# A hybrid decoder step on one core: head sums in two one-pass halves, banks from the plan, a new order of the mixers

## The chip, the core and the metric

The kernel runs on one core of a Trainium2 chip. The metric is the device time of one execution in microseconds (us). The kernel before took 1525.13 us, the median of three runs (1524.78 to 1525.69).

## What is computed

One layer of a decoder over 272 prompt positions (16 meta tokens and 256) and 8 samples of 4 positions, model width 2048, all in fp32. One input projection feeds two parallel groups, RWKV-7 time mixing (16 heads of 64) and retention (4 heads of 256). Their outputs go through one output projection, a residual addition and a SwiGLU FFN of width 5632.

```
z = rms_norm(x) @ w_in                      # RWKV columns | retention columns
# RWKV: kk = k*k_k / |k*k_k| per head;  S = S*w + (S a) b^T + v k^T;  o = S r
#       o = group_norm(o) per head of 64 + sum(r*k*r_k per head) * v;  o * g
# retention: rotary q, k;  o = (q k^T * decay) v + (q S) * decay;  S = g^C S + k^T v
#       o = o * rsqrt(mean(o*o) per head of 256) * silu(g)
h = x + concat(o_rwkv, o_ret) @ w_out
h = h + (silu(hn @ w_gate) * (hn @ w_up)) @ w_down,   hn = rms_norm(h)
```

It returns the final norms of h for prompt and samples, and the new shift, RWKV and retention states of the prompt and of each sample.

## The kernel before, in words

Activations lie with features on the partitions and tokens along the free axis: 304 tokens in the input projection, 288 from the output projection on (the meta tokens are dropped).

**Weights.** All projection weights lie in one stream `big` of 823 tiles of 128 x 512, in the order of use (`sequence`, L109, and `steps`, L129). A tile is loaded by SyncE's queue into one of five buffers (`load`, L658). ScalarE rounds it to fp32r (`wh`, `cast`, L667), and VectorE subtracts to get the rest (`wl`, `rest`, L682). For each block of 128 x 128 TensorE does three one-pass fp32r matmuls: `wh*xh`, `wh*xl`, `wl*xh` (`main`, L688). A job is one output tile of 128 columns: 16 blocks in the input projection, 8 in each half of the output projection, up to 4 in the down projection. Jobs alternate between two PSUM accumulators (`ACC`); a job starts when one is free and its `need` holds.

**Order.** `ORDER` (L55) says in which order the 56 mixer jobs of the input projection come after three jobs for the low-rank inputs: three per RWKV head pair (`p0` to `p7`), six per retention head (`r0` to `r3`), two per gate (`g0` to `g3`). Then come 16 jobs of the output projection on the RWKV half, 16 on the retention half, and the FFN in groups of four tiles (`FSTEP`): gate and up jobs, then 16 down jobs.

**Streams.** All that isn't the weight stream is written as generators (`pair` L980, `bonus`, `by_token`, `inverse`, `units`, `sample` L1302, `pair_out` L1380, `ret` L1462, and the evacuations of jobs). A `Plan` (L325) runs the whole program once as a draft with its own costs of each instruction, and whenever a stream's last result is due by its clock of TensorE it takes that stream's next step, lowest rank first. So it writes out one fixed program order for each engine; the same decisions are replayed for the real program. If the weight stream can't go on, the plan takes the next stream that comes due. In the profile nearly all instructions have the line of the helper that records them, L314.

**Space.** Scratch tiles get places in one SBUF arena, packed by the lifetimes of the draft (`Room`, L505). Six PSUM banks (`mm`) serve the streams in turn (`ps`, L647).

**Limits on concurrency.** Pair p starts when pair p-2 has passed its inverse (`PAIRS`) and pair p-3 is done (`PMAX`). Retention h starts after pair `RSTART[h]` is done.

**The sums over heads.** The matrix `blk` (128 x 128, ones where two rows are of the same head of 64) is the stationary operand of fp32 matmuls that sum over a head: of the squares of k (312 columns, L1014), of r*k scaled by `rk` (288, L1142), of the sample correlations (320, L1338), and for mean and variance of the output (288 each, L1384 and L1392). In retention two fp32 matmuls with a matrix of ones sum the squares (L1594). An fp32 matmul shows in the trace as two records.

**States of the samples.** `sample` ends with the new state of the 8 samples: a transpose, a 512-column fp32 matmul and an addition into the loaded state. `ret` does so for the retention states, four times two fp32r matmuls of 512 columns per head with two VectorE updates each.

Of the kernel before, what the change touches and what calls it, by code (L numbers as in the profile page):

```python
# [68 lines left out]
for _n, _w in [("id", 128), ("blk", 128), ("mar", 256), ("lvl", 2 * 64), ("m16", 64), ("i16", 16), ("h16", 32), ("h32", 128), ("rst", TP),  # L69
               ("bm128", 8), ("ks", 12), ("kss", 4), ("qs", 128), ("own", 256), ("sel", 32)]:  # L70
    CV[_n] = _o
    _o += _w
# [10 lines left out]
ROOM = 33040  # L83
GAP = 56
WIDE = 4200
# [62 lines left out]
def constants():  # L148
# [48 lines left out]
    put("own", np.tile((np.arange(8)[:, None] == bb[None, :]).astype(f).reshape(1, 256), (P, 1)))  # L197
# [121 lines left out]
class Plan:  # L319
# [5 lines left out]
    def __init__(self, nc, rooms, draft, log, keep):  # L325
# [8 lines left out]
        self.streams, self.made = [], 0  # L334
        self.pe = Timed(self, nc.tensor, "PE")
# [5 lines left out]
    def decide(self, f):  # L341

        if not self.draft:
            return self.log.pop(0)
        self.log.append(f())
        return self.log[-1]

# [14 lines left out]
    def book(self, eng, what, a, k):  # L362
# [40 lines left out]
        for x in aps:  # L403
            for room in self.rooms.values():
                room.use(x, self.count, self.begun if eng == "PE" else self.clock[eng] - 400, done)
        for name, box, writes in boxes:
# [181 lines left out]
class Step:  # L588


    def __init__(self, tc, I, O, ctx, rooms, draft, log):
# [8 lines left out]
        self.pp = pool("psum", 8 - ACC, space=bass.MemoryType.PSUM)  # L600
# [3 lines left out]
        if not draft:  # L604
            self.arena = {dt: self.mp.tile([P, r.size + (GAP if dt == F32 else 0)], dt, tag=f"arena_{dt}", name=f"arena_{dt}")
# [3 lines left out]
        self.outs = []  # L609
        self.live = 0  # L610
        self.done = set()

# [10 lines left out]
    def t(self, shape, tag, dt=F32, bufs=None, pool=None):  # L623
        self.n += 1
        if pool is not None:
            ap = pool.tile(shape, dt, tag=tag, name=f"{tag}_{self.n}", **({} if bufs is None else {"bufs": bufs}))
            if tag in ("mm", "acc"):
                self.plan.banks.add(ap.name)
            old = self.tags.setdefault(tag, [])
            old.append(ap.name)  # L630
            n = {"mm": 8 - ACC, "acc": ACC}.get(tag, bufs)
# [15 lines left out]
    def ps(self):  # L647
        return self.t([P, 512], "mm", pool=self.pp)
# [39 lines left out]
    def main(self, jobs):  # L688
# [3 lines left out]
        accs = {}  # L692
        for key, k in steps():
# [3 lines left out]
            if k == 0:  # L697
# [8 lines left out]
                else:  # L706
                    accs[key] = self.first = self.ps()
# [52 lines left out]
    def rsqrt(self, src, scale, eps, floor=None, out=None):  # L760
# [34 lines left out]
    def start(self):  # L795
# [32 lines left out]
        pt = self.ps()  # L828
# [14 lines left out]
    def constants(self):  # L843
# [6 lines left out]
        self.cst = self.t([P, NCV], "cst", pool=self.cp)  # L850
        self.sp.dma_start(self.cst, I["cst"])
# [5 lines left out]
        for a, n in (8, 4), (2, 2), (1, 1):  # L857
            self.dve.tensor_add(xr[:, :n], xr[:, :n], xr[:, a:a + n])
        yield
        yield  # L860
        ssq = self.ps()
# [118 lines left out]
    def pair(self, p, z):  # L980
        cst, act, dve, pe, pool = self.cv, self.act, self.dve, self.pe, self.pool
        blk = cst("blk", P)
# [9 lines left out]
        pw = self.ps()  # L992
        k, r, v, (wh, wl) = z["k"], z["r"], z["v"], z["lora", 0]
        xw, xa = self.xw
        pa = self.ps()
# [7 lines left out]
        rkb = self.t([P, P], "rkb")  # L1003
        dve.tensor_scalar(rkb, blk, self.pv("rk", p), None, op0=ALU.mult)
# [8 lines left out]
        pn = self.ps()  # L1013
        pe.matmul(pn[:, :TP], blk, sq, start=True, stop=True)  # L1014
# [3 lines left out]
        c = self.t([P, TP], "c")  # L1018
# [864 lines left out]
```

## Time and profile before

| | us |
|---|---|
| median of three runs | 1525.13 |
| the profiled execution | 1525.16 |
| its span, first to last instruction | 1523.3 |
| input projection and mixers, with the first output job at | 583.1 |
| first sum of the FFN's norm (fp32, 1 column) | 697.8 |
| last weight matmul | 1510.1 |

In the profile PE is TensorE's matmuls and PEld its weight loads, DVE is VectorE, ACT ScalarE, POOL GpSimd, SP SyncE. A row of the groups gives engine, operation, output and inputs by the program's names (scratch tiles are `arena_dt.float` or `arena_dt.float32r`, the streams' PSUM banks `mm`, the accumulators `acc`), shapes, count, busy time and mean length, then idle time of the engine before them. Matmul records overlap, since matmuls are pipelined; the distance of their starts is what one takes from the stream.

### The profile page before, as it was taken

What the parts mean: (1) busy time and instruction counts of PE and PEld (TensorE: products, weight loads), DVE (VectorE), ACT (ScalarE), POOL (GpSimd) and SP (SyncE); (2) the same over time, 40 slices, a digit from 0 to 9 for tenths busy, and PEclk for the clock granted to TensorE, in tenths of its full rate; (3) what the DMA queues carried; (4) which work ended last, traced back from release to release, by engine and by line L of the source; (5) the groups of instructions that cost most, each with busy time, mean ns of one, the idle gap of its engine ahead of it and who ended that gap; (6) DMA issues with size and microseconds to landing.
All of it is one profiled execution on the core that took longest, in us unless ns stands there. A gap on an engine that the chain in (4) does not pass through costs nothing.

```text
span 1523.3 us, 31919 instructions
## 1 busy us (share of the span) xinstructions
PE 1506.5 (99%) x11446; PEld 1479.4 (97%) x11446; DVE 1087.7 (71%) x2782; ACT 866.4 (57%) x2031; POOL 27.7 (2%) x161
## 2 busy tenths in 40 slices
PE   9999999999999999999999999999999999999997
PEld 8999999999899998999999999999999999999997
DVE  6989789989989877776665655656565656565657
ACT  6775876787886865555444444444444444444446
POOL 1000000000000000000000000000000000000000
PEclk9999999999999999999999999999999999999998
DMA  7655435434544476665566565555656655555663
GB/s 235 177 142 144 126 109 156 126 116 146 163 129 146 167 235 213 210 181 167 167 172 169 172 172 174 166 173 168 170 171 167 177 174 167 172 169 173 169 176 119
DMA packets 136335, 252.33 MB, mean 166 GB/s; under 512 B 15985, under 2 KB 22257, under 8 KB 136177
## 3 DMA queue, kind: packets, MB, share of 16 engines
q1 hardware_dynamic: 136176, 250.29, 55.4%
q8 instruction: 91, 1.49, 0.4%
q14 instruction: 68, 0.55, 0.1%
HBM read 235.95 MB, written 14.28 MB: 164 GB/s over the span
## 4 chain that ended last, share of the span: by engine, by line
PE 89%; DVE 7%; ACT 2%; issue 1%; DMA 0%; SPq 0%; DVEq 0%; ACTq 0%
PE acc L314 79%; PE mm L314 10%; DVE arena_dt.float L314 5%; DVE wl L314 2%; ACT arena_dt.float L314 1%; DMA arena_dt.float<-xT 0%; ACT wh L314 0%; SPq L314 0%; DVE arena_dt.float32r L314 0%; ACT arena_dt.float32r L314 0%; DVE xl L314 0%; ACT xh L314 0%; DVEq L1879 0%; ACT shout L314 0%; DVEq L314 0%
## 5 line engine op out<-in xcount | busy, mean ns | idle before, releaser
L314 PE MATMUL acc<-xh,wh 128*128 128x288 f32 (+2 forms) x2592 | 787.5, 304 | 2.1 <-ACT wh L314 1.3
L314 PE MATMUL acc<-xh,wl 128*128 128x288 f32 (+2 forms) x2592 | 763.2, 294 | 0.3 <-DVE wl L314 0.3
L314 PE MATMUL acc<-xl,wh 128*128 128x288 f32 (+2 forms) x2592 | 760.1, 293 | 0.1
L314 ACT CAST wh<-wr 128x512 fp32r<-128x512 f32 (+1 forms) x827 | 501.2, 616 | 334.6 <-PE acc L314 297.9
L314 DVE TENSOR_TENSOR wl<-wr,wh 128x512 fp32r<-128x512 f32 (+1 forms) x827 | 559.3, 686 | 125.6 <-ACT wh L314 122.7
L314 PEld LDWEIGHTS acc<-xh,wh 128*128 128x128 f32 x2592 | 486.7, 188 | 9.0 <-issue 3.7
L314 PEld LDWEIGHTS acc<-xl,wh 128*128 128x128 f32 x2592 | 486.2, 188 | 4.5 <-issue 1.2
L314 PEld LDWEIGHTS acc<-xh,wl 128*128 128x128 f32 x2592 | 485.3, 187 | 0.9 <-DVE wl L314 0.6
L314 PE MATMUL acc<-arena_dt.float32r,wh 128*128 128x288 f32 x1408 | 273.1, 292 | 0.4 <-ACT arena_dt.float32r L314 0.3
L314 PEld LDWEIGHTS acc<-arena_dt.float32r,wh 128*128 128x128 f32 x1408 | 223.7, 188 | 0.9 <-ACT arena_dt.float32r L314 0.6
L314 PE MATMUL acc<-arena_dt.float32r,wl 128*128 128x288 f32 x704 | 205.6, 292 | 0.0
L314 DVE TENSOR_TENSOR arena_dt.float<-acc,arena_dt.float 128x288 f32<-128x288 f32 (+4 forms) x181 | 72.8, 420 | 161.7 <-PE acc L314 161.4
L314 DVE TENSOR_TENSOR arena_dt.float<-arena_dt.float 128x288 f32<-128x288 f32 (+22 forms) x694 | 175.4, 287 | 11.9 <-ACT arena_dt.float L314 7.6
L314 ACT ACTIVATE arena_dt.float<-arena_dt.float 128x288 f32<-128x288 f32 (+7 forms) x245 | 104.7, 434 | 114.5 <-DVE arena_dt.float L314 112.6
L314 PE MATMUL mm<-arena_dt.float 128*128 128x128 f32 (+7 forms) x1136 | 167.6, 302 | 0.7 <-issue 0.2
L314 DVE TENSOR_TENSOR arena_dt.float<-arena_dt.float,acc 128x288 f32<-128x288 f32 (+1 forms) x210 | 94.6, 451 | 88.3 <-PE acc L314 87.0
L314 PEld LDWEIGHTS mm<-arena_dt.float 128*128 128x128 f32 (+1 forms) x1136 | 141.3, 181 | 11.4 <-issue 3.9
L314 PEld LDWEIGHTS acc<-arena_dt.float32r,wl 128*128 128x128 f32 x704 | 132.1, 188 | 0.0
L314 ACT COPY arena_dt.float<-mm 64x64 f32<-64x64 f32 (+11 forms) x330 | 91.6, 287 | 48.9 <-PE mm L314 39.9
L314 ACT CAST arena_dt.float32r<-arena_dt.float 128x288 fp32r<-128x288 f32 (+4 forms) x73 | 30.5, 423 | 89.4 <-DVE arena_dt.float L314 88.7
L314 ACT COPY arena_dt.float<-arena_dt.float 128x32 f32<-128x32 f32 (+7 forms) x235 | 57.1, 293 | 13.3 <-DVE arena_dt.float L314 11.5
L314 DVE SCALAR_TENSOR_TENSOR arena_dt.float<-arena_dt.float 128x288 f32<-128x288 f32 (+3 forms) x96 | 43.1, 452 | 2.4 <-ACT arena_dt.float L314 0.5
(66 smaller groups left out, 564.8 us busy)
## 6 DMA issues: line engine op xcount, KB each, us to landing
wr<-big SPq DMA_DIRECT2D x823, 256.0 KB, 2.9
arena_dt.float<-s0r SPq DMA_DIRECT2D x16, 512.0 KB, 5.2
out_rts<-arena_dt.float SPq DMA_DIRECT2D x16, 512.0 KB, 4.5
arena_dt.float<-xT SPq DMA_DIRECT2D x4, 576.0 KB, 4.3
arena_dt.float<-lora SPq DMA_DIRECT2D x16, 128.0 KB, 2.7
arena_dt.float<-s0w SPq DMA_DIRECT2D x8, 256.0 KB, 3.0
out_rws<-arena_dt.float SPq DMA_DIRECT2D x8, 256.0 KB, 3.7
out_y<-arena_dt.float SPq DMA_DIRECT2D x7, 288.0 KB, 2.5
```

What stands on the lines that cost most here:

```text
L314: return self._plan.keep(f(*a, **k))
```

## The change

- **Sums.** `blk`, a matrix of ones and a new matrix `cen` (identity minus the mean over the head) are kept in fp32r. Each sum over a head splits its operand with a ScalarE copy and a VectorE subtraction (`split`) and adds two one-pass fp32r matmuls (`total`). `cen` gives the centred output at once. In retention the two squares are added first, and one sum is left. The bonus scales with `rk` in its product, so the scaled copy of `blk` goes.
- **VectorE.** `dp` (decay up to the token before) is taken from shifted columns of `dd`, with three small ScalarE copies for the first columns; two factors move into neighbouring instructions; the reciprocal root loses its shift; `qz` is cleared by GpSimd and filled by two ScalarE copies, without the mask `own`.
- **Banks.** The plan gives out the six PSUM banks: the one that came free first, among those whose announced uses are over.
- **Order.** Pairs and retentions alternate, gates come last. Three pairs may be ahead of their inverse and four alive; retentions 0 and 1 wait for no pair.
- **Late states.** The sample states of the pairs are updated after the output projection with the state loaded again (`sample_state`, rank 99), those of retention heads 2 and 3 after the last retention (`held_states`, rank 98).
- **Stage seams.** The conversions of the mixer outputs for the output projection follow the last input job block by block (`fill`, `refill`). In the last down group the first two jobs are interleaved, and each block waits for its own activation only.

```
-PAIRS = 2
-PMAX = 3
+PAIRS = 3
+PMAX = 4
+HELD = 2
-RSTART = (3, 5, 6, 6)
-ORDER = "p0 p1 g0 p2 r0 p3 p4 g1 p5 r1 p6 g2 p7 g3 r2 r3"
+RSTART = (-1, -1, 6, 6)
+ORDER = "p0 p1 p2 r0 p3 p4 r1 p5 p6 p7 r2 r3 g0 g1 g2 g3"
-ROOM = 33040
-WIDE = 4200
+ROOM = 33008
+WIDE = 4800
...
-    return first + [(key, k) for key in seq[3:] for k in range(extent(key)[0])]
+    rest = [(key, k) for key in seq[3:-KT] for k in range(extent(key)[0])]
+    n = extent(seq[-1])[0] - 1
+    pair = [(key, k) for key in seq[-KT:2 - KT] for k in range(n)] + [(key, n) for key in seq[-KT:2 - KT]]
+    return first + rest + pair + [(key, k) for key in seq[2 - KT:] for k in range(n + 1)]
...
+    put("cen", np.eye(P, dtype=f) - (r[:, None] // 64 == r[None, :] // 64).astype(f) / f(64))
...
+    def bank(self):
+        held = set(self.at.values())
+        return min((b for b in range(8 - ACC) if b not in held), key=lambda b: self.free[b])
...
-    def ps(self):
-        return self.t([P, 512], "mm", pool=self.pp)
+    def ps(self, uses):
+        b = self.plan.decide(self.plan.bank)
+        return self.t([P, 512], f"mm{b}", pool=self.pp, bufs=1, uses=uses)
...   (main)
+            while key[0] == "down" and k not in j.xs:
+                yield False
...
+            if key == last and ("o", k) in self.done:
+                self.fill(k)
...   (rsqrt)
-        dve.tensor_scalar(a.bitcast(I32), x.bitcast(I32), 1, None, op0=ALU.logical_shift_right)
-        yield
-        dve.tensor_scalar(y.bitcast(I32), a.bitcast(I32), -1, 0x5F1FFFF9, op0=ALU.mult, op1=ALU.add)
+        dve.tensor_scalar(y.bitcast(I32), x.bitcast(I32), -0.5, 0x5F1FFFF9, op0=ALU.mult, op1=ALU.add)
...   (pair)
-        pe.matmul(pn[:, :TP], blk, sq, start=True, stop=True)
+        hl = yield from self.split(sq)
+        pn = self.total(self.blk, hl)
...
-        dve.tensor_mul(ra[:, 0, :], kk, dp)
+        dve.tensor_mul(ra[:, 0, 1:], kk[:, 1:], dd[:, :TP - 1])
+        act.copy(ra[:, 0, :1], kk[:, :1])
+        act.copy(ra[:, 0, UB[1]:NP:64], kk[:, UB[1]:NP:64])
+        act.copy(ra[:, 0, NP + 1::5], kk[:, NP + 1::5])
...
+    def split(self, x):
+        hl = self.t([P, 2, x.shape[1]], "hl", F32R)
+        self.act.copy(hl[:, 0, :], x)
+        yield
+        self.dve.tensor_sub(hl[:, 1, :], x, hl[:, 0, :])
+        return hl
+    def total(self, what, hl, uses=1):
+        pt = self.ps(2 + uses)
+        for i in range(2):
+            self.pe.matmul(pt[:, :hl.shape[2]], what, hl[:, i, :], start=not i, stop=i == 1)
+        return pt
...   (sample)
+        self.later.append(self.sample_state(p, sb, d4))
+    def sample_state(self, p, sb, d4):
+        s0 = self.t([P, NB, 64], "s0n")
+        self.sp.dma_start(s0, self.I["s0w"][p])
...   (pair_out)
-        pe.matmul(pm[:, :TO], cst("blk", P), o, start=True, stop=True)
+        hl = yield from self.split(o)
+        pm = self.total(self.cen, hl, 2)
-        dve.scalar_tensor_tensor(o, pm[:, :TO], -1.0 / 64, o, op0=ALU.mult, op1=ALU.add)
-        act.activation(sq, o, AF.Square)
-        pe.matmul(pn[:, :TO], cst("blk", P), sq, start=True, stop=True)
+        act.activation(sq, pm[:, :TO], AF.Square)
+        act.copy(o, pm[:, :TO])
+        hl = yield from self.split(sq)
+        pn = self.total(self.blk, hl)
...   (ret)
+    def held_states(self, h, ks, vt):
+        skh, svh = yield from self.exact(ks, vt)
+        for b2 in range(NB // 2):
+            s0 = self.t([P, 2, 2, RD], "s0n")
+            self.sp.dma_start(s0, self.I["s0r"][h, b2])
+            yield
+            yield from self.new_state(h, b2, s0, skh, svh)
...
-            self.pe.matmul(pt[:, :TO], self.ones, sq[:, e, :], start=e == 0, stop=e == 1)
+        dve.tensor_add(sq[:, 0, :], sq[:, 0, :], sq[:, 1, :])
+        hl = yield from self.split(sq[:, 0, :])
+        pt = self.total(self.all, hl)
...   (ffn_jobs)
-                                need=lambda f=f1 - 1: ("act", f) in self.done))
+                                need=lambda f=f1 - 1 - (f1 == FT): ("act", f) in self.done))
```

More of the change, by code (lines that the diff above doesn't have):

```diff
@@ L405, in book @@
                 room.use(x, self.count, self.begun if eng == "PE" else self.clock[eng] - 400, done)
+        for name in {x.name for x in aps if x.name in self.left}:
+            self.left[name] -= 1
+            assert self.left[name] >= 0, name
+            if not self.left[name]:
+                self.free[self.at.pop(name)] = done
         for name, box, writes in boxes:
@@ L608, in __init__ @@
         pl.outside = {v.name for v in (*I.values(), *O.values())}
-        self.outs = []
+        self.outs, self.later, self.held = [], [], []
         self.live = 0
         self.done = set()
+        self.filled = set()
     def put(self, dst, src):
@@ L692, in main @@
         accs = {}
+        last = [key for key in sequence() if key[0] == "in"][-1]
         for key, k in steps():
@@ L849, in constants @@
         self.sp.dma_start(self.shin, I["shift"])
-        self.cst = self.t([P, NCV], "cst", pool=self.cp)
-        self.sp.dma_start(self.cst, I["cst"])
+        o, n = CV["blk"], NCV - CV["blk"]
+        self.cst = self.t([P, o], "cst", pool=self.cp)
+        self.sp.dma_start(self.cst, I["cst"][:, :o])
+        raw = self.t([P, n], "sums")
+        self.sp.dma_start(raw, I["cst"][:, o:])
+        sums = self.t([P, P + n], "sums", F32R, pool=self.cp)
+        self.act.copy(sums[:, :P], self.ones)
+        self.all, self.blk, self.cen = (sums[:, c * P:(c + 1) * P] for c in range(3))
         for g in range(0, KT, 4):
@@ L858, in constants @@
             self.dve.tensor_add(xr[:, :n], xr[:, :n], xr[:, a:a + n])
+        self.act.copy(sums[:, P:], raw)
         yield
         yield
-        ssq = self.ps()
+        ssq = self.ps(2)
         self.pe.matmul(ssq[:, :T], self.ones, xr[:, 0, :], start=True, stop=True)
@@ L1336, in sample @@
             yield
-        pt = self.ps()
-        pe.matmul(pt[:, :320], cst("blk", P), cf, start=True, stop=True)
+        hl = yield from self.split(cf)
+        yield
+        pt = self.total(self.blk, hl)
         yield
@@ L1512, in ret @@
         dve.tensor_mul(pr, pt[:, :RMW], rm)
-        qz = self.t([P, 2, NB, 32], "qz")
         for d in range(2):
-            dve.tensor_mul(qz[:, d], qh[:, d, None, :].to_broadcast([P, NB, 32]),
-                           cst("own", 256).rearrange("p (b c) -> p b c", c=32))
-        pt = self.ps()
+            act.copy(qz[:, d, :, :4], four(qh[:, d]))
+        pt = self.ps(7)
         for d in range(2):
@@ L1557, in ret @@
                 act.copy(qo, pt[:, :RD])
[L1559 to L1576 removed]
+            if now:
+                for b2 in range(2 * g, 2 * g + 2):
+                    yield from self.new_state(h, b2, s0s[b2], skh, svh)
+        if not now:
+            self.held.append(self.held_states(h, ks, vt))
+            yield
         ot = self.t([P, 2, TO], "ot")
@@ L1591, in ret @@
         yield
-        pt = self.ps()
-        for e in range(2):
-            pe.matmul(pt[:, :TO], self.ones, sq[:, e, :], start=e == 0, stop=e == 1)
+        dve.tensor_add(sq[:, 0, :], sq[:, 0, :], sq[:, 1, :])
+        yield
+        hl = yield from self.split(sq[:, 0, :])
+        yield
+        pt = self.total(self.all, hl)
         yield
@@ L1600, in ret @@
         self.done.add(("ret", h))
+        if h == RH - 1:
+            self.plan.add(self.rest_of(self.held), 98)
         yield from self.ret_out(h)
@@ L1671, in bridge, with fill, refill @@
     def bridge(self, n=BRIDGE):
-        pt = self.ps()
+        pt = self.ps(n)
         for _ in range(n):
             self.pe.matmul(pt[:, :P], self.ones, self.ones, start=True, stop=True)
+    def fill(self, k):
+        if k not in self.filled:
+            self.filled.add(k)
+            xh, xl = self.xf[k]
+            self.act.copy(xh, self.os[k])
+            self.dve.tensor_sub(xl, self.os[k], xh)
+    def refill(self):
+        for k in range(8, KT):
+            while ("o", k) not in self.done:
+                yield
+            self.fill(k)
+            yield
     def out_jobs(self, half):
@@ L1697, in f @@
                     self.done.add("hs")
+                    self.plan.add(self.rest_of(self.later), 99)
                 yield from self.sumsq(self.ssq2, hm, m == 0)
@@ L1748, in g @@
                 acts[f - f0] = hl[:, 0, :], hl[:, 1, :]
-                if last:
-                    self.done.add(("act", f))
+                self.done.add(("act", f))
             return g
```

189 lines of the change are left out of this document (99 added, 90 removed).

## The prediction

> **What bounds the kernel now.** I read the page's engine table first, then the table of windows by stage, then the groups by form, and last the timeline around single sums. The page, of the one profiled execution:
>
> ```profile
> span 1523.3 us, 31919 instructions
> ...
> PE 1506.5 (99%) x11446; PEld 1479.4 (97%) x11446; DVE 1087.7 (71%) x2782; ACT 866.4 (57%) x2031; POOL 27.7 (2%) x161
> ```
>
> TensorE is busy throughout, but a matmul record also counts pipelined time, so the share alone proves little. The windows say more: the length, then busy time and instructions of PE, weight load, VectorE, ScalarE and GpSimd, then the granted clock, DMA share and rate.
>
> ```profile
> 50.00:550.00 500.00, 498.47 (x3696) 480.68 (x3694) 444.68 (x1577) 381.60 (x1127) 22.26 (x122) 1.00 0.48 143
> 550.00:583.00 33.00, 31.85 (x228) 28.20 (x226) 19.68 (x46) 19.39 (x48) 0.00 (x0) 1.00 0.75 262
> ```
>
> ```profile
> 700.00:1480.00 780.00, 780.00 (x6054) 780.00 (x6053) 467.92 (x842) 338.96 (x594) 0.00 (x0) 1.00 0.59 171
> ```
>
> In the FFN one one-pass matmul of 288 columns starts every 780/6054 = 0.1288 us, without a break, at clock 1.00. Nothing can be won there but fewer passes. In the mixer stage (50 to 583) PE shows 1.53 + 1.15 = 2.7 us of idle time, while VectorE is at 444.68/500 = 89%. So in both stages the passes of TensorE are the time: what is taken off PE comes off the end one for one, as long as its next instruction is always ready. A cheaper VectorE buys nothing by itself; a VectorE that falls behind would cost.
>
> **The sums over heads.** Five per pair go from one fp32 matmul to two one-pass halves: the norm of k (312 columns), the bonus (288), the sample correlations (320), mean and variance in the output (288 each). Per retention head two fp32 matmuls with ones become an addition and one sum in halves. Their groups by form, two records to an fp32 matmul:
>
> ```profile
> L314 PE MATMUL mm<-arena_dt.float,cst 128*128 128x288 f32 x32 | 10.8, 418 | 0.2 <-ACT arena_dt.float L314 0.2
> ...
> L314 PE MATMUL mm<-arena_dt.float,cst 128*128 128x320 f32 x16 | 5.7, 436 | 0.0
> L314 PE MATMUL mm<-arena_dt.float,cst 128*128 128x312 f32 x16 | 5.6, 432 | 0.0
> L314 PE MATMUL mm<-arena_dt.float 128*128 128x288 f32 x16 | 5.5, 423 | 0.1
> ...
> L314 PE MATMUL mm<-arena_dt.float,ones 128*128 128x288 f32 x16 | 4.5, 406 | 0.0
> ```
>
> So 16 output sums, 8 of 320, 8 of 312, 8 bonuses, 8 of ones. The means overlap one another and are no prices. The price is how far a sum puts off the passes behind it, which the timeline shows (start, length, instruction):
>
> ```profile
> 213.66 0.57 PE L314 MATMUL mm<-arena_dt.float32r 128*128 128x288 f32 x3
> 214.06 0.65 PE L314 MATMUL mm<-arena_dt.float,cst 128*128 128x288 f32 x2
> 214.33 0.52 PE L314 MATMUL acc<-xh,wh 128*128 128x304 f32 x1
> 214.69 0.30 PE L314 MATMUL acc<-xl,wh 128*128 128x304 f32 x1
> 214.83 0.30 PE L314 MATMUL acc<-xh,wl 128*128 128x304 f32 x1
> ```
>
> ```profile
> 86.76 0.70 PE L314 MATMUL mm<-arena_dt.float,cst 128*128 128x320 f32 x2
> 87.05 0.54 PE L314 MATMUL acc<-xh,wh 128*128 128x288 f32 x1
> 87.43 0.29 PE L314 MATMUL acc<-xl,wh 128*128 128x288 f32 x1
> ```
>
> ```profile
> 608.68 1.13 PE L314 MATMUL mm<-arena_dt.float,ones 128*128 128x288 f32 x4
> 609.44 0.51 PE L314 MATMUL acc<-xh,wh 128*128 128x288 f32 x1
> 609.79 0.29 PE L314 MATMUL acc<-xl,wh 128*128 128x288 f32 x1
> ```
>
> From the sum's start to the second pass behind it, less the one pass between:
> - 288 columns: 214.69 - 214.06 - 0.14 = 0.49. Two halves: the three one-pass matmuls of 288 from 213.66 to 214.06 take 0.133 each, the FFN 0.129, so 0.26. Saves 0.23, times 24 = 5.5 us.
> - 320: 87.43 - 86.76 - 0.13 = 0.54 against 2 x 0.129 x 320/288 = 0.29. Saves 0.25, times 8 = 2.0. 312 lies between: 0.53 against 0.28, again 0.25, times 8 = 2.0.
> - Ones: 609.79 - 608.68 - 0.13 = 0.98 against 0.26. Saves 0.72, times 4 = 2.9.
>
> Sum: 12.4 us, all on PE, all where PE has no spare time. Mixing the two kinds of matmul costs nothing that shows: the 0.49 holds both changes of kind.
>
> The Trainium skill (FP8 and Floating Point Precision, TensorE Precision Notes) says that true FP32 takes four passes through the array. An estimate by that page would be 4 x 0.129 = 0.515 for the sum whose row gives 0.49, and 13.8 us saved in all instead of 12.4. The trace nearly agrees, at 3.8 passes; the rows decide.
>
> **What the sums add elsewhere.** Each sum now needs a ScalarE copy to the rounded half and a VectorE subtraction before PE may start. Off the path; these rows price VectorE's side:
>
> ```profile
> L314 DVE TENSOR_TENSOR wl<-wr,wh 128x512 fp32r<-128x512 f32 (+1 forms) x827 | 559.3, 686 | 125.6 <-ACT wh L314 122.7
> ...
> L314 DVE TENSOR_TENSOR arena_dt.float<-arena_dt.float,acc 128x288 f32<-128x288 f32 (+1 forms) x210 | 94.6, 451 | 88.3 <-PE acc L314 87.0
> ...
> L314 DVE TENSOR_TENSOR arena_dt.float32r<-arena_dt.float,arena_dt.float32r 128x288 fp32r<-128x288 f32 (+4 forms) x72 | 31.8, 441 | 1.1 <-ACT arena_dt.float32r L314 0.7
> ...
> L314 DVE SCALAR_TENSOR_TENSOR arena_dt.float<-arena_dt.float,mm 128x512 f32<-128x512 f32 x32 | 20.5, 682 | 0.3 <-PE mm L314 0.2
> ```
>
> Five subtractions of 0.44 = 2.2 us a pair come in; six VectorE instructions of a like size go out (scaled mask, dp, the factor of ta, the centring, the shift in two reciprocal roots). I take that as even, so "less VectorE work" is mainly work that leaves the mixer: half of the 32 state updates (heads 2 and 3, 16 x 0.68 = 11 us), plus two instructions of that size per pair (8 x 1.36 = 11 us). VectorE falls from 445 to about 423 of those 500 us. A sum's operands come some 0.9 us later, about 4.5 us a pair. That is hidden: between the last columns of pair 7 and the output projection there are now 20 jobs (two retentions, four gates) of 48 passes, 20 x 48 x 0.129 = 124 us, where there were 14. Eight pairs, two at a time, in 500 us make 125 us for a pair at most. Were the cover gone, the 4.5 us would show once, for the last pair.
>
> **Starts and ends of stages.** At the first output job all eight x tiles were converted at once; in the last FFN group PE waited for the last activation:
>
> ```profile
> 583.09 0.40 PE L314 MATMUL acc<-xh,wh 128*128 128x288 f32 x1 [0.79 <-ACT xh L314]
> 583.58 0.40 PE L314 MATMUL acc<-xl,wh 128*128 128x288 f32 x1
> ```
>
> ```profile
> 1485.43 0.29 PE L314 MATMUL acc<-arena_dt.float32r,wl 128*128 128x288 f32 x1
> 1486.06 0.89 PE L314 MATMUL acc<-arena_dt.float32r,wh 128*128 128x288 f32 x2 [0.34 <-ACT arena_dt.float32r L314]
> 1486.79 0.29 PE L314 MATMUL acc<-arena_dt.float32r,wl 128*128 128x288 f32 x1
> ```
>
> At 583 the loss is 0.79 + (0.49 - 0.13) = 1.15 us. The conversions now follow the last input job tile by tile; I take 1.0 back (bounds 0 and 1.15). At 1486 it is (0.63 - 0.13) + (0.73 - 0.26) = 0.97. With two jobs interleaved, 18 passes stand ahead of the one that needs the last activation, instead of nine, 1.16 us more, so that stall goes. What is late next is the third job: it takes the first one's accumulator, free 0.29 (a pass) + 0.45 (the addition, above) = 0.74 after that job's last pass starts, and is due after 4 x 0.13 = 0.52. Net 0.97 - 0.22: I take 0.7 (bounds 0, if another VectorE instruction of 0.68 stands in front, and 0.97).
>
> **Order, banks, early retention.** These move waits, and the trace of before has few to move. At 1486 0.34 us of idle stood for 0.97 lost, so the 1.53 us shown in 50 to 550 can stand for up to 4.4. I take 0: the changes can remove at most 4.4, and with a third pair and retention from the start more short chains feed PE, each of which can come late by as much; the other end is the VectorE rival below.
>
> **Sample states late.** The matmuls are the same and cost PE the same, in the FFN. Added are reloads on SP's queue: eight of s0w, and eight of s0r for heads 2 and 3.
>
> ```profile
> arena_dt.float<-s0r SPq DMA_DIRECT2D x16, 512.0 KB, 5.2
> ...
> arena_dt.float<-s0w SPq DMA_DIRECT2D x8, 256.0 KB, 3.0
> ```
>
> That is 6.3 MB on queues whose share in the FFN is 0.59. Behind a reload that waits for its place in SBUF stand the weight loads; five buffers of 12 passes are 5 x 1.55 us, so SP may be held about 6 us before PE starves. I take 0; bounds 0, and 0.5 us for each of 16 reloads, 8 us (5.2 + 3.0 of landing against those 6 us leaves 2 at worst, so 0 is the nearer end).
>
> **The sum.** The profiled execution took 1525.16 us, 1.9 around its span, and the median of the runs is 1525.13, so they stand for each other. 1525.1 - 12.4 - 1.0 - 0.7 = 1511.0 us.
>
> **The rivals.**
> - *VectorE becomes the bound while three pairs and retentions 0 and 1 run together (slower).* Up to pair 7's last columns (39 of 59 input jobs, so some 39/59 x 533 = 350 us) 1.5 times the pair work may be wanted at once. Of 445 us in 50 to 550 at most 3696/12 x 0.686 = 211 are weight halves; the other 234 are 0.47 of the time, at 1.5 times 0.70, with the weights 1.12. That puts VectorE 0.12 x 350 = 42 us behind. It decides once the lag exceeds the slack of the other accumulator, one job of 48 passes or 6.2 us. If half of the lag reaches PE, 1511 + 21 = 1532. For it: 89% now. Against: 22 us leave the mixer, and streams that lag give way to input jobs as long as there are any.
> - *The halves save nothing, because weight loads set the pace (no change).* Of the weight loads:
>
> ```profile
> L314 PEld LDWEIGHTS acc<-xh,wh 128*128 128x128 f32 x2592 | 486.7, 188 | 9.0 <-issue 3.7
> ```
>
> Each sum has two loads before and after. At 0.188 a load a sum in halves takes 0.38 when nothing overlaps; if the present 0.49 is likewise set by loads and drains that stay, only the ones sums gain, 8 loads or 1.5 us: 1525.1 - 1.5 = 1523.6. Against: a pass starts every 0.129 us, so loads of 0.188 overlap.
>
> The Trainium skill (Perfetto Trace Analysis, Identifying the Most-Contended Engine) judges TensorE's headroom by weight-load busy share and not by matmul busy share; at 97% that rule speaks against the change. The FFN's spacing of 0.129 says that this share is no limit here.
> - *Late states collide with the weight stream.* 1511 + 8 = 1519.
> - *The short waits go too.* 1511 - 4.4 = 1506.6.
>
> **How the numbers follow.** The forecast has 0.67: with halves at 0.133 the sum is 0.4 smaller, and the two small terms span 0 to 2.1, the unknown waits about 2 either way, so its own range is 1508 to 1515. VectorE 0.09, weight loads 0.06, late states 0.09, short waits 0.09. About 0.2%, 3 us, is what a measurement can tell from no change. Faster: 0.67 + 0.09 + 0.09 = 0.85; same 0.06; slower 0.09. The range 1506 to 1519.5 takes in all but the first two rivals.
>
> **What would show it.** Right: the fp32 groups with cst and with ones over 288 are gone, 44 x 2 one-pass records stand in their place 0.13 apart; 700 to 1480 still gives 0.129 a pass outside the late matmuls; PE idle in 50 to 550 stays near 1.5 us; no 0.79 us ahead of the first output job. Wrong: PE waiting in the mixer on VectorE's results or on accumulators for more than 10 us in all, a first output job that waits for pair 7, or ScalarE's weight copies waiting on wr loads beside s0n reloads.

## The result: 2.7% slower, and where the profile after puts it

The changed kernel took 1565.49 us, the median of four runs (1561.24 to 1570.62), against 1525.03 us for the kernel before: a ratio of 1.0266 (95% interval 1.0235 to 1.0297). The forecast was 1511.0 with a range to 1519.5. The result lies 54 us above the forecast, on the slower side, which had a chance of 0.09. The profiled execution has a span of 1563.9 us, 40.6 more than before.

One remark for the numbers below: two runs of the first experiment (1539.6 and 1540.5 us) and one of the fourth (1586.9 us) are not compared, since the profiled ones among them show FFN passes 3.5% further apart than the profile of after, and the rows of the first experiment's profile are used up to 675 us only, where nothing else is said.

The page after, busy times and the chain that ended last:

```profile
PE 1511.4 (97%) x11438; PEld 1480.9 (95%) x11438; DVE 1092.1 (70%) x2768; ACT 881.5 (56%) x2109; POOL 31.5 (2%) x165
...
PE 82%; DVE 6%; ACT 4%; DMA 4%; issue 2%; SPq 1%; DVEq 0%; ACTq 0%
```

Here the share of a busy engine misleads. PE is still at 97%, and only the chain shows the change: 18% of it is now not PE, with VectorE, ScalarE and DMAs in it. Before, 11% was not PE (89% PE, 7% DVE, 2% ACT, DMA 0%).

The windows by stage, of after, with the columns as in the prediction:

```profile
50.00:550.00 500.00, 476.64 (x3562) 463.25 (x3560) 429.60 (x1528) 366.63 (x1081) 29.04 (x146) 0.99 0.43 135
550.00:675.00 125.00, 115.45 (x855) 107.33 (x854) 82.70 (x174) 68.00 (x157) 0.21 (x1) 0.97 0.64 221
...
800.00:1480.00 680.00, 680.00 (x5278) 680.00 (x5278) 409.51 (x735) 293.12 (x513) 0.00 (x0) 1.00 0.58 171
```

And of before, the one that the prediction did not show and that is needed here:

```profile
550.00:675.00 125.00, 123.66 (x934) 117.42 (x933) 91.35 (x192) 71.66 (x154) 0.00 (x0) 1.00 0.66 216
```

The last row of after shows the FFN untouched: 5278 passes in 680 us, 0.1288 each. The loss is ahead of it. In the 500 us of the mixers PE has 500 - 476.64 = 23.4 us of idle time, where before it had 1.5, and it got 134 records less done (3562 instead of 3696), although each sum is now shorter. VectorE is less busy than before (429.60 instead of 444.68), so by this row it is not the bound. In 550 to 675 idle grows from 1.3 to 9.6 us. By the timeline the first output job starts at 606.9, not 583.1 (+23.8), and the last weight matmul at 1551.3, not 1510.1 (+41.2). The mixers lose more than those 23.8, since the shorter sums and the late states took work out of them; in the 17.4 behind lie the late states, which moved there, and the idle time of the output projection.

What do they wait for? The waits of after (us in total, times, longest):

```profile
ACT wh L317 <- DMA wr<-big: 37.9, 26, 4.1
...
PE mm L317 <- ACT arena_dt.float L317: 11.2, 9, 2.4
...
ACT arena_dt.float32r L317 <- DMA arena_dt.float<-lora: 8.3, 5, 3.4
```

The same waits of before:

```profile
ACT wh L314 <- DMA wr<-big: 5.9, 5, 1.5
...
PE mm L314 <- ACT arena_dt.float L314: 1.1, 3, 0.6
...
ACT arena_dt.float32r L314 <- DMA arena_dt.float<-lora: 0.5, 1, 0.5
```

ScalarE waits 37.9 us for weight tiles (5.9 before), and PE's short matmuls of the streams wait 11.2 us for ScalarE (1.1). But the weights were late to be asked for, rather than slow to come: from issue to landing they take 2.9 us by the page, before and after. The waits of SP's queue, before and then after:

```profile
SPq L314 <- DVE wl L314: 902.6, 700, 13.0
SPq L314 <- DVE arena_dt.float L314: 205.3, 98, 16.6
...
SPq L314 <- PE mm L314: 8.2, 7, 3.5
```

```profile
SPq L317 <- DVE wl L317: 784.4, 638, 6.4
SPq L317 <- DVE arena_dt.float L317: 239.0, 99, 16.6
SPq L317 <- PE mm L317: 41.5, 15, 11.2
...
SPq L317 <- ACT arena_dt.float L317: 32.6, 11, 9.0
```

A wait for `wl` is the good one: the queue is ahead, and all five weight buffers are full. It fell from 902.6 to 784.4. What grew are waits for an engine to be done with a scratch tile, so that a load can take its place.

One such place can be followed from end to end. The chain around 364 us, start and length:

```profile
364.37 3.78 DMA out_rts<-arena_dt.float
...
368.17 3.22 DMA arena_dt.float<-lora
...
371.42 0.02 ACT arena_dt.float32r L317
```

And the timeline of the engines and of SP's queue in the same stretch, with PE's next matmul:

```profile
368.17 0.34 SPq L317 DMA_DIRECT2D arena_dt.float<-lora  x1
368.18 0.44 ACT L317 COPY arena_dt.float<-arena_dt.float 128x8 f32<-128x8 f32 x3 [3.06 <-DMA out_rts<-arena_dt.float]
368.25 0.54 DVE L317 TENSOR_TENSOR arena_dt.float<-acc,arena_dt.float 128x272 f32<-128x272 f32 x2 [2.56 <-DMA out_rts<-arena_dt.float]
...
368.61 0.38 SPq L317 DMA_DIRECT2D wr<-big  x1
```

```profile
369.00 0.49 PE L317 MATMUL mm<-arena_dt.float 128*128 128x128 f32 x2 [2.38 <-ACT arena_dt.float L317]
...
369.59 0.41 PE L317 MATMUL acc<-xh,wh 128*128 128x290 f32 x1
369.79 0.45 PE L317 MATMUL acc<-xl,wh 128*128 128x290 f32 x1
370.04 0.44 PE L317 MATMUL acc<-xh,wl 128*128 128x290 f32 x1
...
372.45 1.01 PE L317 MATMUL mm<-arena_dt.float32r 128*128 128x312 f32 x4
```

A retention state is being stored (`out_rts`). By these waits, three things have been given places inside it: a tile that ScalarE writes (3.06 us of waiting), one that VectorE writes (2.56), and a `lora` load on SP's queue. Behind that load stand the weight tiles, whose next ones go out at 368.61. PE stands for 2.38 us, and then its passes come 0.24 us apart (369.79 to 370.04), not 0.13. The clock says why:

```profile
364.00:369.00 5.00, 2.62 (x21) 2.38 (x19) 1.81 (x5) 1.88 (x8) 0.48 (x5) 1.00 0.80 278
369.60:373.00 3.40, 3.40 (x17) 3.40 (x16) 2.00 (x7) 2.21 (x8) 0.00 (x0) 0.50 0.96 289
```

The column after GpSimd's is the granted clock: 0.50 for the 3.4 us behind the stall. The Trainium skill (TensorE: Matmul & The Clock Gate, Part 1: The HAM clock gate) says that TensorE falls to half its clock after about 3.4 us of idleness and needs as much work to come back. The trace agrees on the half clock and on the 3.4 us of work; the idleness ahead of it was shorter than the page's, 2.38 us in one piece, and the measurement decides. Over the whole span the mean granted clock fell from 0.997 to 0.992, worth (0.008 x 1563.9) - (0.003 x 1523.3) = 8 us at the most.

So the reading, still to be tested, was: nothing that an engine does got slower, the clock behind stalls apart; places in the scratch arena are given from one tile to the next with no time between, and whoever gets the place waits.

### The profile page after: what moved, and what is told of

The parts are those of the page before. It is cut to its first block, busy times and chain, and to the rows that moved or that the text cites. A ratio compares the mean times of both kernels' runs of the same rounds, so it can differ in the third digit from the quotient of the medians.

```text
span 1563.9 us, 32063 instructions
## 1 busy us (share of the span) xinstructions
PE 1511.4 (97%) x11438; PEld 1480.9 (95%) x11438; DVE 1092.1 (70%) x2768; ACT 881.5 (56%) x2109; POOL 31.5 (2%) x165
## 4 chain that ended last, share of the span: by engine, by line
PE 82%; DVE 6%; ACT 4%; DMA 4%; issue 2%; SPq 1%; DVEq 0%; ACTq 0%
PE acc L317 72%; PE mm L317 10%; DVE arena_dt.float L317 4%; ACT arena_dt.float L317 3%; DVE wl L317 2%; DMA arena_dt.float<-s0r 1%; ACT wh L317 1%; DMA wr<-big 1%; DMA arena_dt.float<-lora 1%; SPq L317 1%; DVE xl L317 0%; DVE arena_dt.float32r L317 0%; DMA arena_dt.float<-s0w 0%; DMA arena_dt.float<-xT 0%; ACT arena_dt.float32r L317 0%
## 5 line engine op out<-in xcount | busy, mean ns | idle before, releaser
L317 PE MATMUL mm<-arena_dt.float 128*128 128x128 f32 (+7 forms) x1120 | 171.2, 310 | 27.9 <-ACT arena_dt.float L317 11.2
L317 DVE TENSOR_TENSOR arena_dt.float<-arena_dt.float 128x32 f32<-128x32 f32 (+23 forms) x658 | 159.2, 279 | 16.3 <-ACT arena_dt.float L317 6.6
L317 ACT ACTIVATE arena_dt.float<-arena_dt.float 128x288 f32<-128x288 f32 (+7 forms) x229 | 97.1, 432 | 106.5 <-DVE arena_dt.float L317 104.6
L317 ACT COPY arena_dt.float<-mm 64x64 f32<-64x64 f32 (+11 forms) x338 | 95.0, 290 | 47.3 <-PE mm L317 36.0
L317 ACT CAST arena_dt.float32r<-arena_dt.float 128x288 fp32r<-128x288 f32 (+6 forms) x117 | 49.7, 430 | 93.9 <-DVE arena_dt.float L317 83.0
L317 ACT COPY arena_dt.float<-arena_dt.float 128x8 f32<-128x8 f32 (+8 forms) x267 | 62.4, 282 | 32.4 <-DVE arena_dt.float L317 27.8
L317 DVE TENSOR_TENSOR arena_dt.float32r<-arena_dt.float,arena_dt.float32r 128x288 fp32r<-128x288 f32 (+6 forms) x116 | 51.7, 448 | 5.1 <-ACT arena_dt.float32r L317 4.5
```

The source lines that it names most:

```text
L317: return self._plan.keep(f(*a, **k))
```

## The experiments

**The theories.** The packer (`Room.place`) tries wanted distances in time between two uses of one place, 2000 ns first, then less, until the tiles fit; a tile that finds no place at that distance takes the place with the longest one. Its own figure for what it could not give, `lack`, is the sum over the tiles of what the distance to the nearest neighbour falls short of 800 ns; below I call it the shortfall. For before it is 50 us, packed with 2000 ns; for after 331 us, packed with 0. (The times in it are those of the plan, not of the chip.) Two things lie behind it. More is alive at once (a third pair, retentions from the start, the halves). And the diff lifts `WIDE`, the limit of the rounded arena, from 4200 to 4800, and lowers `ROOM` by 32: the rounded arena grows from 3536 to 4544 columns, and the fp32 arena's limit falls from 29504 to 28464.

- Theory A, places: the packing without slack costs the time. The same program with other addresses is fast.
- Rival B, VectorE: the streams lag because more work is wanted at once. Addresses change nothing.
- Rival C, late states: the reloads hold up SP's queue. Without them, or with them on another queue, the time is back.
- A further rival, banks or order: the plan's new choices themselves make PE wait.

The expectations use these letters; D, where it appears, is the view that doing the states late gains time of its own.

**A looser packing of the changed kernel.** The edit moves addresses and nothing else; the shortfall falls to 102 us. (The last number is how often the packer tries again with the tile that did not fit put first.)

```
-WIDE = 4800
-FREE, GAPS, TRIES = 800.0, (2000.0, 1000.0, 500.0, 200.0, 50.0, 0.0), 12
+WIDE = 4400
+FREE, GAPS, TRIES = 800.0, (800.0, 0.0), 60
```

> The changed kernel with another packing of SBUF alone: the fp32r room may take 4400 columns instead of 4800, so 304 more are left for fp32, and places are chosen with 800 ns between the last use of one tile and the first of the next (by the plan's clock) instead of none. The plan, the order on every engine and the instructions are the same; only addresses differ. The packing's own shortfall (what is missing to 800 ns, summed over tiles) falls from 331 us to 102 us; the kernel before has 50. Theory A (waits for places in SBUF that were packed without slack): the 53 us of lost PE time fall by more than half, to 1520-1545 us; ScalarE's weight copies wait for wr loads less than the 38 us they do now. Theory B (VectorE and ScalarE queues too full with three pairs and two early retentions): 1560-1570, no change. Theory C (late states and their reloads): no change outside 575-775 us, at best 1555.

Measured: 1514.2 and 1514.7 us in the runs compared, a ratio of 0.992 (0.990 to 0.994) to before, and better than the range that theory A gave. Its windows:

```profile
50.00:550.00 500.00, 497.56 (x3775) 487.13 (x3774) 441.49 (x1564) 384.95 (x1128) 22.53 (x115) 1.00 0.46 144
550.00:675.00 125.00, 124.27 (x968) 120.95 (x967) 97.82 (x199) 72.99 (x154) 0.20 (x1) 1.00 0.75 251
```

PE's idle time in the mixers is 2.4 us again, and VectorE does more in the same time (441.49), because nothing holds it up. ScalarE's waits for weight tiles between 50 and 675 us fall from 34.8 to 9.4 us. Instructions and order are those of the changed kernel: both profiles have the same 11438 matmuls in the same order, and the one that starts at 800.1 us after starts at 748.8 here. These 51.3 us are as much as the whole difference between 1565.5 and 1514.4. So neither B, nor the banks, nor the order, nor C, the late states, makes the slowdown by itself: they are all still there.

**The loads on GpSimd's queue.** The loads into scratch tiles (`lora`, `s0w`, `s0r`, `rmask`, the residual) are issued by GpSimd, with the tight packing kept. The weights, the constants and inputs at the start, and all stores stay on SyncE's queue.

```
+        self.side = Timed(self, nc.gpsimd, "SP")
...
-        self.sp.dma_start(s0, self.I["s0w"][p])
+        self.plan.side.dma_start(s0, self.I["s0w"][p])
...   (the six other loads in the same way)
```

> The changed kernel with seven kinds of loads into scratch tiles (lora, s0w, both s0r, rmask, residual x) issued on GpSimd's queue instead of SyncE's, so that a load that waits for its place in SBUF no longer stands ahead of the weight loads. Same plan, same packing. Theory A1 (spacing hurts through SyncE's queue, the weight loads behind a waiting load): ScalarE's waits for wr loads fall from 38 to under 10 us and the time to 1530-1550. Theory A2 (spacing hurts directly, where ScalarE, VectorE and the loads themselves wait for places): 1555-1570. Theory B (full VectorE and ScalarE queues): no change, 1560-1570. GpSimd's memsets now stand behind waiting loads and could cost some us under each.

Measured: 1557.79 us (1555.89 to 1561.41), ratio 1.0214 (1.0194 to 1.0234), about 8 us better than after: in the range for waits that do not go through the queue, and far from the 1530 to 1550 for the queue alone. Its waits:

```profile
ACT arena_dt.float32r L317 <- DMA arena_dt.float<-lora: 22.5, 12, 4.0
...
ACT wh L317 <- DMA wr<-big: 14.0, 9, 3.2
```

The weight tiles come in time more often (14.0 instead of 37.9), but the loads that were taken off the queue wait for their places all the same, and their users with them (22.5 instead of 8.3). SyncE's queue was thus only one way by which a late place reaches PE. That most of the loss goes other ways, such as the ScalarE and VectorE waits at 368 us, is likely but not shown: GpSimd's memsets now stand behind loads that wait, and what that costs was not separated.

**The kernel before, packed without slack.** Every tile of the old program, the old order, the old limits; only the wanted distance is 0. The shortfall of the fp32 arena rises from 50 to 290 us.

```
-FREE, GAPS, TRIES = 800.0, (2000.0, 1000.0, 500.0, 200.0, 50.0, 0.0), 12
+FREE, GAPS, TRIES = 800.0, (0.0,), 12
```

> The kernel before, with places in SBUF chosen without any wanted spacing (the list of wanted gaps is 0 alone). Plan, order and instructions are those of before; only addresses differ; the packing's shortfall goes from 50 to 290 us. Theory A (places without slack): slower, 1535-1575 us, with ScalarE waiting for wr loads well above the 6 us of before. Theories B (full queues) and C (late states): 1525, no change.

Measured: 1559.49 us (1556.79 to 1563.03), ratio 1.0218 (1.020 to 1.0236). Its windows and waits:

```profile
50.00:550.00 500.00, 481.62 (x3508) 460.60 (x3507) 429.87 (x1530) 363.32 (x1071) 28.72 (x150) 0.99 0.43 135
550.00:675.00 125.00, 121.30 (x886) 113.14 (x885) 87.30 (x192) 75.58 (x182) 0.21 (x1) 1.00 0.60 204
```

```profile
ACT arena_dt.float32r L314 <- DMA arena_dt.float<-lora: 13.9, 7, 4.0
...
PE mm L314 <- ACT arena_dt.float L314: 11.1, 11, 3.8
...
ACT wh L314 <- DMA wr<-big: 7.6, 5, 3.1
```

Addresses alone make the old kernel 33 us slower, with the idle time of PE (18.4 and 3.7 us) in the same stages as in the changed kernel. This is the strongest of the runs, since nothing of the change is in it. One expected sign did not come: ScalarE's waits for weight tiles are 7.6 us, hardly more than the 5.9 of before. Here the late places reach PE by ScalarE's tiles (11.1 us instead of 1.1) and by `lora` loads (13.9 instead of 0.5), and not by weight tiles that were asked for late. Matched one by one, the matmuls are 34 us behind those of before at 800 us and 38 at the end; the 4 us between lie in the FFN, whose passes are 0.1296 us apart (680/5247), for a reason not known.

**The limit of 4400 without the slack.** The first experiment changed three things: the limit, the distance and the number of tries. This one keeps its limit of 4400 and its 60 tries, and packs with 0 (shortfall 305 us).

```
-WIDE = 4800
-FREE, GAPS, TRIES = 800.0, (2000.0, 1000.0, 500.0, 200.0, 50.0, 0.0), 12
+WIDE = 4400
+FREE, GAPS, TRIES = 800.0, (0.0,), 60
```

> The first experiment's kernel (fp32r room of 4400 columns) with the wanted gap set to 0 alone: the same columns, the same plan and order, but places follow each other without slack. The packing's shortfall is 305 us (changed kernel 331, first experiment 102). Theory A (slack between uses): slow again, 1545-1565. Theory A' (the 304 columns themselves matter, whatever the slack): as the first experiment, 1514.

Measured: 1559.45 to 1564.01 us in the runs compared, ratio 1.0239 (1.0222 to 1.0256), as slow as after. The distance decides, and the columns matter only in that they leave no room for it.

**More room.** The rows of the x and activation tiles are made 12 columns narrower, which frees 384 columns for the arena, and the packing has 2000 ns at first (shortfall 92 us).

```
-XW = T + 16
-ROOM = 33008
-WIDE = 4800
-FREE, GAPS, TRIES = 800.0, (2000.0, 1000.0, 500.0, 200.0, 50.0, 0.0), 12
+XW = T + 4
+ROOM = 33392
+WIDE = 4400
+FREE, GAPS, TRIES = 800.0, (2000.0, 1200.0, 800.0, 0.0), 60
```

> The changed kernel with room of 4400 columns for fp32r, rows of the x and activation tiles cut from 320 to 308 columns (384 columns more for scratch), wanted gap 2000 ns: shortfall 92 us, the least found for this plan. Theory A: as fast as the first experiment's undisturbed runs or a little faster, 1510-1515. If addresses of the x tiles matter for TensorE's reads: passes of the FFN no longer 0.129 us apart, and the time above 1520.

Measured: 1539.79 us (1539.43 to 1541.72), ratio 1.0097 (1.008 to 1.0113). A miss for theory A; what came is the other case of the expectation, passes further apart and a time above 1520. The windows:

```profile
50.00:550.00 500.00, 496.45 (x3756) 486.96 (x3755) 438.91 (x1555) 382.97 (x1123) 23.50 (x117) 1.00 0.48 145
...
800.00:1480.00 680.00, 680.00 (x5150) 680.00 (x5149) 400.53 (x716) 286.43 (x500) 0.00 (x0) 1.00 0.57 167
```

The mixers are good (3.6 us idle). But the FFN does 5150 passes in 680 us, 0.1320 each instead of 0.1288, with PE without a break and the clock at 1.00. Over the FFN's 780 us that is 19 us. The narrow rows, or the addresses that move with them, may be what slows TensorE's own pace; but other kernels with rows of 320 show a slower pace too (0.1296 above, 0.1333 below), so the cause is not shown. The kernel still serves as the base for two of the runs below.

**The late states early again,** on the roomier kernel: the pairs' state updates follow at once, and all four retention heads update in their streams (the limit of the rounded arena is 4800 here).

```
-HELD = 2
+HELD = 4
...
-        self.later.append(self.sample_state(p, sb, d4))
+        yield from self.sample_state(p, sb, d4)
```

> The changed kernel with all sample states updated at once and none late (no reloads), row pitch 308, shortfall 113 us, so the slack is about that of the first experiment. Theory C (late states and their reloads cost): faster than the first experiment's 1514, 1505-1512. Theory D (late states take VectorE work and room out of the mixers and so pay): slower, about 1520-1525; the plan itself has 8 us more idle PE.

Measured: 1560.62 us (1559.55 to 1563.71), ratio 1.0233 (1.0218 to 1.0249), 20.8 us above the roomier kernel with late states, at nearly the same shortfall (113 us).

```profile
50.00:550.00 500.00, 484.68 (x3620) 471.29 (x3619) 435.80 (x1541) 384.71 (x1164) 23.43 (x121) 0.99 0.49 145
550.00:675.00 125.00, 118.22 (x876) 111.64 (x875) 87.81 (x188) 73.56 (x174) 0.00 (x0) 0.99 0.61 202
```

PE idles 15.3 us in the first stretch and 6.8 in the second, where the roomier kernel has 3.6 and 0.4. So C has the wrong sign, and D fits: the late states gain some 21 us in this order, and most of it is idle time of PE that is gone (15.3 + 6.8 against 3.6 + 0.4, 18.1 us). The size is rough: 8 us of idle PE stand in the plan itself, the limit of the rounded arena differs, and two packings of like shortfall can be 9 us apart, as the third packing below shows. A reason is at hand, though not shown: in the mixers VectorE has 436 of 500 us to do, in the FFN 0.59 of the time.

**The sums in fp32 again,** in the looser packing (shortfall 69 us): one fp32 matmul for each sum, no split.

```
-        sums = self.t([P, P + n], "sums", F32R, pool=self.cp)
+        sums = self.t([P, P + n], "sums", pool=self.cp)
...   (split: returns x; total:)
-        for i in range(2):
-            self.pe.matmul(pt[:, :hl.shape[2]], what, hl[:, i, :], start=not i, stop=i == 1)
+        self.pe.matmul(pt[:, :hl.shape[1]], what, hl, start=True, stop=True)
```

> The changed kernel in the first experiment's packing manner (room 4400, gap 800; shortfall 69 us) with the 44 sums over heads as one fp32 matmul each, without the split into halves (the single retention sum and the centring matrix stay). By the prices of the prediction the halves save 24 x 0.23 + 8 x 0.25 + 8 x 0.25 + 4 x 0.23 = 10.4 us on TensorE, so this kernel should take 1514 + 10 = 1524. Rival (weight loads set the pace): 1514, no change.

Measured: 1557.57 us (1555.42 to 1559.91), ratio 1.021 (1.0195 to 1.0226). Its windows, to be set beside the first experiment's:

```profile
50.00:550.00 500.00, 492.95 (x3682) 477.80 (x3680) 419.75 (x1511) 366.65 (x1078) 22.85 (x115) 1.00 0.48 144
550.00:675.00 125.00, 121.85 (x934) 117.66 (x927) 91.98 (x186) 67.59 (x142) 0.00 (x0) 1.00 0.70 228
...
800.00:1480.00 680.00, 680.00 (x5102) 680.00 (x5102) 397.04 (x710) 283.75 (x497) 0.00 (x0) 1.00 0.58 165
```

The two programs differ in the sums, and the plan, which knows their cost, orders the streams a little differently; both kinds of sum leave two records. At 550 us this kernel is 3775 - 3682 = 93 records behind, 12.3 us at 0.132, and at 675 another 34 (4.5 us). Of these 16.8 us PE is idle 4.6 + 2.4 us longer; the other 9.8 are near the 10.4 expected for longer sums. The expected time, 1524, was missed. Most of the miss is the FFN, which ran at 0.1333 us a pass here (680/5102), of which below. The first experiment's profile has the same pace there (5103 passes), so the two spans can be set side by side: 1558.1 - 1537.9 = 20.2 us, twice what was expected. The halves thus save PE about what was forecast; why some 10 us more come on top, the 7 us of idle time among them, was not followed.

**A third packing.** The same plan once more, with other addresses for nearly every tile, at a shortfall of 98 us.

```
-WIDE = 4800
-FREE, GAPS, TRIES = 800.0, (2000.0, 1000.0, 500.0, 200.0, 50.0, 0.0), 12
+WIDE = 4400
+FREE, GAPS, TRIES = 800.0, (1000.0, 0.0), 60
...   (the orders of packing; the rest of the line is as it was)
+            for key in (lambda n, a, b, *_: (-n * (b - a + 1) ** 2, a), lambda n, a, b, *_: (-n, a), ...
```

> The changed kernel with the same instructions and the same plan, packed a third way: limit 4400 for the rounded arena, one more order of packing (by size times the square of the lifetime) and a wanted distance of 1000 ns. The shortfall of distance comes to 98 us, about that of the packing with 4400 columns before (102), but nearly every tile lies somewhere else. If the distance between two uses of a place is what cost the time, this is again 1512 to 1517, faster than before by 0.7 to 0.9 per cent, with fewer than 20 ScalarE waits of the weight copies for wr loads. If instead that one packing happened to have good addresses (banks or partitions that do not collide), this lies anywhere between 1515 and 1565.

Measured: 1523.22 us (1520.29 to 1523.98), ratio 0.9974 (0.9963 to 0.9985). Better than before and 42 us better than after, but 6 us above the range expected if distance is all; by the letter of the expectation it falls to the other case, a first packing with lucky addresses, which had 1515 to 1565. Two packings of nearly the same shortfall are 9 us apart, so the shortfall does not say everything.

```profile
50.00:550.00 500.00, 495.45 (x3753) 485.49 (x3752) 439.18 (x1556) 382.18 (x1122) 22.97 (x116) 1.00 0.48 144
...
800.00:1480.00 680.00, 680.00 (x5278) 680.00 (x5277) 408.51 (x732) 294.17 (x514) 0.00 (x0) 1.00 0.59 171
```

PE idles 4.6 us in the mixers, and ScalarE's waits for weight tiles come to 19.7 us, half of those of after. The FFN is at 0.1288. The shortfall is a rough measure at least because it counts a tight place off the chain like one on it. Whether other properties of an address play a part in the 9 us was not tested. For the rest, chance would hardly sort the packings so well: the three without distance (after, the old kernel packed again, the limit of 4400) are the slow ones, and the three with it (before, the first experiment, this one) the fast ones.

**The banks in turn,** as in the kernel before, on the roomier kernel (shortfall 114 us; the limit of the rounded arena is 4800 here).

```
-        b = self.plan.decide(self.plan.bank)
-        return self.t([P, 512], f"mm{b}", pool=self.pp, bufs=1, uses=uses)
+        self.turn = (getattr(self, "turn", -1) + 1) % (8 - ACC)
+        return self.t([P, 512], f"mm{self.turn}", pool=self.pp, bufs=1)
```

> The slack kernel with rows of 308 (compare with that one, 1539.8), but the six PSUM banks taken in turn as in the kernel before, not given out by the plan. The plan's own clock of TensorE then ends 2.4 us later, and the shortfall of distance is 114 us, where it was 92. If the banks have no price of their own here: 1540 to 1545. If giving them out by the plan is what feeds three pairs: PE waits for banks in the mixer, and this is 1552 or more.

Measured: 1542.95 us (1542.76 to 1543.39), ratio 1.011 (1.0094 to 1.0125), 3 us above the roomier kernel with intervals that overlap. The banks are worth 3 us or nothing, as far as two packings can tell.

## Why the prediction was wrong

- **The step that failed** is "Order, banks, early retention": "I take 0: the changes can remove at most 4.4, and with a third pair and retention from the start more short chains feed PE". The other end was sought in VectorE alone. The step priced a denser program by PE's idle time in the old one, and that idle time was small because the old tiles could be packed with 2000 ns wanted between two uses of a place. What the denser program does to the places was not asked. The `ROOM` and `WIDE` lines of the diff, 1040 columns taken from the fp32 scratch, got no price at all. The runs showed in its place: same program, tight packing 1565.5, looser packing 1514.4, so 51 us; for the old program 33 us.
- **The head sums** (12.4 us): their price on PE was right. In the third packing a sum in halves takes 0.26:

```profile
210.64 0.43 PE L317 MATMUL mm<-arena_dt.float32r,sums 128*128 128x288 f32 x2
210.90 0.30 PE L317 MATMUL acc<-xh,wh 128*128 128x288 f32 x1
211.04 0.29 PE L317 MATMUL acc<-xl,wh 128*128 128x288 f32 x1
```

  The second pass behind it starts 211.04 - 210.64 - 0.14 = 0.26 later than without it, as priced, against 0.49 before. The rival that weight loads take this back is refuted, by this row and by the sums in fp32, which cost 20.2 us.
- **The first output job** (1.0 us): it starts without a break, so the whole 1.15 came back.

```profile
606.94 0.30 PE L317 MATMUL acc<-xh,wh 128*128 128x288 f32 x1
607.07 0.30 PE L317 MATMUL acc<-xl,wh 128*128 128x288 f32 x1
```

- **The last down group** (0.7 us): what is late next was named rightly, the third job waiting for the first one's accumulator.

```profile
1529.19 0.29 PE L317 MATMUL acc<-arena_dt.float32r,wl 128*128 128x288 f32 x1
1529.64 0.53 PE L317 MATMUL acc<-arena_dt.float32r,wh 128*128 128x288 f32 x2 [0.16 <-DVE arena_dt.float L317]
1530.01 0.30 PE L317 MATMUL acc<-arena_dt.float32r,wl 128*128 128x288 f32 x1
```

  The loss is (0.45 - 0.13) + (0.37 - 0.26) = 0.43 against 0.97, so 0.54 came back.
- **VectorE** as the new bound, the rival that stood for the slower side, is refuted by the first experiment, although VectorE's work did not fall to the 423 us that were forecast for the mixers (441.49 there). It had the right sign for the wrong reason.
- **Late states** were put at 0 with a loss of 8 as the bound. On the roomier kernel they gain 21: moved work was counted, but not what early states do to the mixers in the new order.
- **What would show it wrong** caught it in part. PE's idle time in 50 to 550 did not stay near 1.5 us (23.4), and ScalarE's copies waited on `wr` loads (37.9). But PE's waits there on VectorE's results come to 6.6 us, under the 10 named, and 8.5 are on ScalarE, which was not named; and in the case followed the load in front of the weights was a `lora` load of the mixers, no late reload.

With places to spare, the sum comes near: 1514.4 measured in the first experiment against 1511.0. Part of that is luck. If the 21 us of the late states hold there too, then with the sums (12.4) and the seams (1.15 + 0.54) the time should be 1490, and some 24 us went the other way, in the new order, the third pair, the early retentions or the places that are still tight. Two terms put at 0 would then have nearly cancelled; this is an estimate, since no run adds them one at a time. The Trainium skill (Perfetto Trace Analysis, Identifying Performance Opportunities, Optimization Strategy) says that consistent bubbles on the engine that should be saturated can mean that SBUF or PSUM has no room for the next tile. The runs agree that room in SBUF was the cause, with 33 and 51 us, though the gaps here are of several kinds and not one that repeats; the same rule would have asked the right question of the diff.

Two things stay open. Order, early retention and the third pair were not run apart from the rest, so their own gain or loss is unknown. And which of the tight places carry the loss was followed in single cases only, so no share is given for each.

The version to keep is the changed kernel in the looser packing of the first experiment: 1514.4 us in the runs compared, 0.8% below before. The third packing is slower in these, but its seven runs all lie between 1520.3 and 1524.0.

## What to carry to other kernels

A planned kernel that reuses SBUF by lifetime has a resource that no busy share shows: the time between two uses of a place. Before a change that keeps more alive, compare the packing's slack before and after, and price a tight place as a wait for the last reader or store of the tile that was there, with everything queued behind it. When a trace shows waits everywhere and no slower engine, change only the addresses: a run of the old program with a tight packing separates places from everything else.

## What the runs showed of the hardware

- A stall of 2.38 us was followed by 3.4 us at a granted clock of 0.50 and passes 0.24 us apart, so this stall cost about half as much again (the 12 passes from 369.59 to 372.45 took 2.86 us; at 0.134 they take 1.61, so 1.25 us more).
- In the three kernels whose x and activation rows are 308 columns apart the FFN's passes took 0.1320 us, and 0.1288 in before, after and the third packing, with rows of 320, at clock 1.00 and with PE never idle: 5150 to 5157 passes in the same 680 us against 5278. Whether it is the row length, the addresses that move with it or something else was not tested.
- With rows of 320, the same passes came 0.1333 us apart throughout the FFN of the profiled executions of the first and the fourth experiment and of the one with fp32 sums, again at clock 1.00, and 0.1296 apart in the old kernel packed without slack. The third packing has 0.1288 with the same plan as the first and the fourth. The cause is not known.
